# A streaming-encoder layer on one core: weight sums made by adding DMAs are issued one at a time over three stages, and a gate uses Silu in place of Sigmoid and a multiplication

## The chip, the cores and the metric

The kernel runs on one core of a Trainium2 chip. The metric is the device time of one execution in microseconds (us). Lower is better. Names of engines in the profile: PE is TensorE (matmuls; PEld is its weight load), DVE is VectorE, ACT is ScalarE, POOL is GpSimd, and SP is SyncE, which issues most DMAs.

## The reference, cut to what matters

One layer over 1024 frames of width 1024. The change touches how two things are computed: the weighted sums that feed the projections `W_out` and `w_ffn_down`, and the SwiGLU gate.

```python
merged = (jax.nn.sigmoid(gate_a) * (oa @ w_branch_a[li])
          + jax.nn.sigmoid(gate_b) * (ob @ w_branch_b[li]))
x = x + merged @ w_out[li]
h2 = rmsnorm(x, norm_ffn_g[li])
x = x + (jax.nn.silu(h2 @ w_ffn_gate[li]) * (h2 @ w_ffn_up[li])) @ w_ffn_down[li]
h3 = rmsnorm(x, norm_ple_g[li])
x = x + jax.nn.sigmoid(h3 @ w_ple_gate[li]) * (p[li] @ w_ple_proj[li])
```

## The kernel before

Everything is held with features on the partitions and frames along the free axis, in tiles of 128 x 512 or 128 x 1024. A float32 product is made of three fast products: each operand is split into a high part (a cast to `fp32r`, on ScalarE) and a low part (the rest, a subtraction on VectorE or GpSimd), and a block product is hi x hi, lo x hi and hi x lo. In the names below, `whi`/`wlo` and `wh`/`wl` are the high and low parts of weights, `wr` the raw weights as loaded, `q` a sum or difference of weight blocks, `pm` a PSUM bank, `t` a 128 x 512 temporary from a ring of eight, `s` a 128 x 1024 slot, `rb` the row of norm factors, `d` a tile in device memory.

The stages in order of time: norm, recurrent mixer, attention, gate units, branches, output projection, gate/up units of the feed-forward, its down projection, embedding. From the gate units on, products of 2 x 2 blocks are made by Strassen's scheme, seven products in place of eight. A *unit* of the gate units or of the gate/up units (`strassen`, line 1429) is seven products of 12 matmuls of 128 x 512 each; the result of the fourth goes onto the bank of the second, so the sum `u2 = p1 + b2` on VectorE must have read that bank first (lines 1457 to 1465).

The seven products need seven forms of the weights. For a unit, `strassen_weights` (line 1386) makes those of the *next* unit as side work: sums and differences `q` on VectorE, high parts on ScalarE, low parts on GpSimd and (one of them) on VectorE. It is a generator; after each product the unit takes one step of it. There are 12 gate-unit column blocks in six units (`gate_units`, line 800; they make the sigmoids of `gate_a` and `gate_b`), and 22 gate/up units: unit 0 is `first_part` and `second_part`, units 1 to 21 are the loop in `ff_pairs` (line 1515). Even units make the gate, odd ones the up half.

A gate unit's four results pass through `unit_gate` (line 1372): VectorE multiplies by the norm row into a slot `s` (twice its half), ScalarE makes the Sigmoid in a temporary `t`, and GpSimd multiplies twice, `s*t` and then `s*rb`. In the up unit VectorE multiplies the result in (`unit_up`).

For `W_out` and `w_ffn_down` the sums of weights are made in device memory, without an engine reading them: `dma_sums` (line 1053) first copies blocks of the weight into spill tiles (SP queue, during attention), then issues DMAs from the GpSimd queue that add a second block onto the copy in transit (`accum_op`). There are 8 such additions for `W_out` (`self.osum`) and 24 for `w_ffn_down` (`self.wsum`). Each `next()` of these generators issues one. Those of `osum` go out in the gate units, two to a unit, until they are used up; those of `wsum` in the up units 1, 3, 5, ... of the feed-forward, three to a unit, until they are used up in unit 15. `drain` issues what is left before the sums are used.

What sets the order: the framework schedules an engine's instructions freely, except those that go through `self.V`, `self.A`, `self.G`, `load` or `mul`, which are kept in program order on their engine (`Pinned`, line 45). The additions in transit go through `self.G`. The low parts of ordinary weights (`unit_piece`, line 118) and the additions of the two branch products (`branches`, line 893) are free on GpSimd. In `branches` eight weight tiles are used, one for 48 matmuls; weights are made ready three tiles ahead.

Of the kernel before, what the change touches and what calls it, by code (L numbers as in the profile page):

```python
# [14 lines left out]
ALU = mybir.AluOpType  # L15
# [40 lines left out]
class Trunk:  # L56
    def __init__(self, tc, d, out):
        self.tc, self.nc, self.d, self.out = tc, tc.nc, d, out
        self.V = Pinned(self, self.nc.vector, "dve")
        self.A = Pinned(self, self.nc.scalar, "act")  # L60
        self.G = Pinned(self, self.nc.gpsimd, "pool")
        self.n = self.turn = 0
        self.by_turns = False
        self.ahead = 2
        self.done = set()
        self.prev = {}
# [9 lines left out]
    def load(self, out, ap):  # L76
        return self.order(self.nc.sync.dma_start(out, ap), "sp")
# [40 lines left out]
    def unit_piece(self, unit, a, b):  # L118
        hi, lo, raw, ap = unit
        c = slice(a, b)  # L120
        self.load(raw[:, c], ap[:, c])
        self.nc.scalar.copy(hi[:, c], raw[:, c])  # L122
        self.turn += 1
        rest = self.nc.vector if self.by_turns and self.turn % 2 else self.nc.gpsimd
        rest.tensor_tensor(lo[:, c], raw[:, c], f32(hi[:, c]), ALU.subtract)  # L125

    def weights(self, n=1, ahead=AHEAD):
# [672 lines left out]
    def gate_units(self):  # L800

        V, A = self.V, self.A
        h0, h1 = slice(0, HALF), slice(HALF, T)
        self.gd = [self.spill() for _ in range(2 * KC)]
        self.kept = []
        for k in (2, 3):
            self.mix_load(k, self.slot(), [self.stmp(), self.stmp()])
        self.strassen_load()
        side = chain(self.strassen_weights(V), self.mix_sums(2), self.mix_sums(3))
        ts, self.gates = self.gates, []  # L810
        for c, t in enumerate(ts):
            A.activation(t, t, AF.Sigmoid)
            self.kept.append((self.gd[c], t))
        for c in range(2, PLAIN):
            (w,) = self.weights(1, ahead=PLAIN - 1 - c)
            for half in range(2):
                if c == PLAIN - 1 and half:
                    drain(side)
                    side = self.mix_last()
                stream = self.feature(w, self.u, half, piece=2)  # L820
                while True:
                    try:
                        next(stream)
                    except StopIteration as e:
                        ps = e.value
                        break
                    next(side, None)
                    if c == 2 and half == 0 and self.kept:
                        self.keep_heads(self.ob, self.obd, [2, 3])
                        self.gate_keep()  # L830
                    next(side, None)
                self.gate_done(c, half, ps)
                next(side, None)
        drain(side)
        u, t = self.u, self.t32
        cut = lambda pair, h: [x[:, h] for x in pair]
        four = range(4)
        self.sops = [
            [cut(u[2 * k + 1], h1) for k in four], [cut(t[k], h1) for k in four],
            [cut(self.t1[k // 2], slice(k % 2 * HALF, k % 2 * HALF + HALF)) for k in four], [cut(t[k], h0) for k in four],  # L840
            [cut(u[2 * k], h1) for k in four], [cut(u[2 * k + 1], h0) for k in four], [cut(u[2 * k], h0) for k in four]]
        units = (2 * KC - PLAIN) // 2
        for n in range(units):

            def side():
                more = self.strassen_weights() if n + 1 < units else self.branch_first()
                if n == 0:
                    yield
                    yield
                next(more, None)  # L850
                if n + 2 < units:
                    self.strassen_load()
                yield
                for i, _ in enumerate(more):
                    if i % 2:
                        next(self.osum, None)
                    yield

            self.strassen(lambda c, half, ps: self.gate_done(PLAIN + 2 * n + c, half, ps), side(), early=n == 0)
            yield 0  # L860
        self.gate_keep()

    def branch_load(self, src):
        raws = []
# [28 lines left out]
    def branches(self):  # L893
        nc, V = self.nc, self.V
        self.m = {}
        gates, load = self.bgates, self.gate_load

        def tile(c, half):
            key = f"B{c % 2 + 1}{half + 1}", c // 4
            if key not in self.m:  # L900
                self.m[key] = self.slot()
            return self.m[key][:, c // 2 % 2 * HALF:c // 2 % 2 * HALF + HALF]

        src = self.osrc
        for dd in range(4):
            (w,) = self.weights()
            load()
            if dd == 1:
                raws = self.branch_load(self.obd)
                late = []  # L910
            for i in range(2):
                c = 2 * dd + i
                for half in range(2):
                    hs = slice(half * HALF, half * HALF + HALF)
                    ps = yield from self.feature(w, src, half, off=i * HALF)
                    V.tensor_tensor(tile(c, half), ps, gates[c][:, hs], ALU.mult)
                    yield 2592
                if dd > 1:
                    late.append(self.split(raws[len(late)]))
        src = late  # L920
        for dd in range(4):
            (w,) = self.weights()
            load()
            for i in range(2):
                c = 2 * dd + i
                g = gates[KC + c]
                for half in range(2):
                    hs = slice(half * HALF, half * HALF + HALF)
                    ps = yield from self.feature(w, src, half, off=i * HALF)
                    V.tensor_tensor(g[:, hs], ps, g[:, hs], ALU.mult)  # L930
                    (nc.gpsimd if dd < 3 else V).tensor_tensor(tile(c, half), tile(c, half), g[:, hs], ALU.add)
                    yield 2592
            if dd == 1:
                self.branch_sums(0)
            if dd == 2:
                self.x, self.xd = [], [None] * KC
                for c in range(KC):
                    x = self.slot()
                    self.load(x, self.d["x"][c])
                    self.x.append(x)  # L940
                self.m_order = [(b, i) for _, b in self.KINDS for i in range(2)]
                self.m_ready = []
                self.m_split()
# [150 lines left out]


    def out_proj(self):
        drain(self.osum)
        split, ready = self.m_split, self.m_ready

        def operand(b, i):  # L1100
            got = ready.pop(0)
            if len(ready) < 2:
                split()
            return got

        split()
        self.branch_sums(1)
        self.by_turns = True
        yield from self.passes(4, operand, self.added(lambda c: self.x[c]), self.ffn_side())
        self.by_turns = False  # L1110
# [261 lines left out]
    def unit_gate(self, c, half, ps):  # L1372
        V, A, G = self.V, self.A, self.G
        g = self.gu[c]
        hs = slice(half * HALF, half * HALF + HALF)
        s = self.stmp()
        V.tensor_tensor(g[:, hs], ps, self.rb[:, hs], ALU.mult)
        A.activation(s, g[:, hs], AF.Sigmoid)
        G.tensor_tensor(g[:, hs], g[:, hs], s, ALU.mult)
        G.tensor_tensor(g[:, hs], g[:, hs], self.rb[:, hs], ALU.mult)  # L1380

    def unit_up(self, c, half, ps):
        hs = slice(half * HALF, half * HALF + HALF)
# [131 lines left out]
    def ff_pairs(self):  # L1515
# [5 lines left out]
        for n in range(1, units):  # L1521
# [3 lines left out]
            def side():  # L1525
# [6 lines left out]
                yield  # L1532
                for i, _ in enumerate(more):
                    next(keep, None)
                    if n % 2 and i % 2 == 0:
                        next(self.wsum, None)
                    yield
                drain(keep)

# [5 lines left out]
    def down_plan(self):  # L1545

        n = NFF // 2
        self.aorder = [(b, i, min(D, n * HALF - i * D)) for _, b in self.KINDS for i in range(STEPS)]
        drain(self.wsum)
        self.plan_weights(self.quad_plan(self.d["dw"], n, self.sums) + self.worder2)  # L1550
        self.anext, self.araw, self.aready = 0, [], []

# [366 lines left out]
def drain(stream):  # L1919
    while True:  # L1920
        try:
            next(stream)
        except StopIteration as e:
            return e.value
# [114 lines left out]
```

## Time and profile before

| | |
|---|---|
| median of three runs | 1601.0 us (1599.59 to 1601.37) |
| the profiled execution | 1600.6 us, its span 1598.8 us, mean granted clock 0.994 |
| attention ends, gate units begin | about 518 us into the span |
| branches, output projection | about 667 to 755, 755 to 860 |
| gate/up units | about 860 to 1290 |
| down projection, embedding | about 1290 to 1510, 1510 to 1599 |

In a row of a group of instructions stand line, engine, operation, output<-inputs with shapes, the count, then busy us and mean ns of one, then the idle time of the engine just before them with what ended it. In a row of the timeline stand start and length in us, and in brackets the idle time before. An "issue" as releaser means that the engine waited for nothing that the profile shows. Many instructions share line 53, which is the helper that pins them; they are told apart by their tiles. In a row of a stretch stand the stretch, then busy us and the number of instructions for PE, PEld, DVE, ACT and POOL, the granted clock of PE as a share of full speed, the mean busy share of the DMA engines, and GB/s.

### The profile page before, as it was taken

Reading aid. Unit: us, or ns where it says so; the run is one execution under the profiler, and the core shown is the slowest. Engines: PE = TensorE matmul, PEld = TensorE weight load, DVE = VectorE, ACT = ScalarE, POOL = GpSimd, SP = SyncE. Lnnn points to the kernel's source line nnn. Section 1 sums busy time; section 2 is a strip of 40 time slices with the busy share of each in tenths; the row PEclk is TensorE's granted clock in tenths of the full one; section 3 lists DMA queues with packets and bytes.
Section 4 is the critical chain, followed back from the end, with each engine's and each line's share of the span. In section 5 each row is a group of like instructions: output and inputs, shape, how many; then the busy total and the mean of one; then the engine's idle time right before and its main releaser. Section 6 shows DMA issues by size and latency. Waiting matters only on the chain.

```text
span 1598.8 us, 21535 instructions
## 1 busy us (share of the span) xinstructions
PE 1559.1 (98%) x8224; PEld 1312.8 (82%) x8224; DVE 1171.8 (73%) x1685; ACT 636.9 (40%) x1057; POOL 712.5 (45%) x397
## 2 busy tenths in 40 slices
PE   8999999999999999999999999989999999999997
PEld 6998998888888888888888777877788888888886
DVE  5656656378786876436898889889998876765677
ACT  5222221177676633322566222222222234445462
POOL 3422221313121053335313777767777764544453
PEclk9999999999999999999999999999999999999998
DMA  5101000362523475754335555555543278885434
GB/s 187 53 28 50 31 28 27 112 185 80 177 82 118 170 174 130 271 203 184 114 136 211 137 133 141 123 132 135 129 132 103 78 267 325 294 283 184 133 116 164
DMA packets 83527, 230.38 MB, mean 144 GB/s; under 512 B 8928, under 2 KB 9568, under 8 KB 82912
## 3 DMA queue, kind: packets, MB, share of 16 engines
q1 hardware_dynamic: 76880, 213.26, 39.1%
q0 software_dynamic: 6400, 15.73, 6.1%
q8 instruction: 64, 1.05, 0.3%
q14 instruction: 39, 0.32, 0.1%
q10 hardware_dynamic: 144, 0.02, 0.0%
HBM read 179.43 MB, written 81.00 MB: 163 GB/s over the span
## 4 chain that ended last, share of the span: by engine, by line
PE 75%; DVE 15%; issue 3%; ACT 1%; DMA 1%; POOL 1%; SPq 0%; DVEq 0%; POOLq 0%; ACTq 0%
PE pm L82 72%; DVE s L53 8%; DVE q L53 3%; PE pm L85 3%; DVE t L53 2%; DVE m L53 1%; DMA d<-s 1%; DVE pm L53 0%; ACT s L53 0%; POOL wl L125 0%; DMA wr<-in_fm 0%; ACT wh L122 0%; POOL m L555 0%; ACT m L53 0%; DVE wlo L53 0%
## 5 line engine op out<-in xcount | busy, mean ns | idle before, releaser
L82 PE MATMUL pm<-s,wh 128*128 128x512 f32 (+1 forms) x1712 | 531.9, 392 | 6.6 <-ACT wh L122 5.3
L82 PE MATMUL pm<-s,whi 128*128 128x512 f32 x1568 | 487.8, 392 | 14.4 <-DVE t L53 14.4
L125 POOL TENSOR_TENSOR wl<-wr,wh 128x1024 fp32r<-128x1024 f32 (+2 forms) x108 | 266.9, 2476 | 396.7 <-ACT wh L122 383.4
L82 PEld LDWEIGHTS pm<-s,wh 128*128 128x128 f32 x1712 | 319.9, 189 | 73.4 <-ACT wh L122 5.9
L82 PEld LDWEIGHTS pm<-s,whi 128*128 128x128 f32 x1568 | 295.1, 189 | 81.6 <-DVE t L53 20.7
L82 PE MATMUL pm<-s,wl 128*128 128x512 f32 (+1 forms) x856 | 333.9, 390 | 0.0
L53 DVE TENSOR_TENSOR s<-s,s 128x512 f32<-128x512 f32 (+3 forms) x228 | 273.2, 1230 | 79.2 <-ACT s L53 41.7
L82 PE MATMUL pm<-s,wlo 128*128 128x512 f32 x784 | 307.0, 392 | 0.7 <-POOL wlo L53 0.7
L82 PE MATMUL pm<-wh,s 128*128 128x256 f32 (+1 forms) x896 | 237.6, 340 | 0.0
L122 ACT CAST wh<-wr 128x1024 fp32r<-128x1024 f32 (+2 forms) x114 | 115.0, 1010 | 271.8 <-PE pm L82 139.4
L82 PEld LDWEIGHTS pm<-s,wl 128*128 128x128 f32 x856 | 161.3, 188 | 33.7 <-POOL wl L125 0.6
L82 PEld LDWEIGHTS pm<-s,wlo 128*128 128x128 f32 x784 | 148.0, 189 | 33.0 <-POOL wlo L53 1.6
L82 PEld LDWEIGHTS pm<-wh,s 128*128 128x128 f32 x896 | 154.4, 190 | 14.0
L53 DVE TENSOR_TENSOR t<-pm,t 128x512 f32<-128x512 f32 x138 | 94.5, 685 | 79.7 <-PE pm L82 75.2
L82 PE MATMUL pm<-wl,s 128*128 128x256 f32 (+1 forms) x448 | 147.5, 329 | 0.4 <-POOL wl L125 0.4
L53 POOL TENSOR_TENSOR wlo<-wr,whi 128x512 fp32r<-128x512 f32 (+1 forms) x53 | 113.4, 2142 | 73.4 <-PE pm L82 67.2
L53 ACT CAST whi<-q 128x512 fp32r<-128x512 f32 (+1 forms) x81 | 61.4, 758 | 153.2 <-DVE q L53 113.1
L53 ACT CAST s<-s 128x1024 fp32r<-128x1024 f32 (+1 forms) x94 | 90.1, 980 | 63.4 <-DVE s L53 34.7
L53 POOL TENSOR_TENSOR wlo<-q,whi 128x512 fp32r<-128x512 f32 x52 | 84.5, 1625 | 50.4 <-DVE t L53 17.8
L53 POOL TENSOR_TENSOR s<-s,t 128x512 f32<-128x512 f32 x44 | 73.1, 1662 | 66.6 <-ACT t L53 66.6
L82 PEld LDWEIGHTS pm<-wl,s 128*128 128x128 f32 x448 | 85.4, 191 | 5.9 <-POOL wl L125 0.6
L53 ACT ACTIVATE t<-s 128x512 f32<-128x512 f32 x44 | 27.8, 632 | 142.8 <-DVE s L53 139.0
(145 smaller groups left out, 1929.7 us busy)
## 6 DMA issues: line engine op xcount, KB each, us to landing
s<-d SPq DMA_DIRECT2D x67, 512.0 KB, 6.1
d<-s SPq DMA_DIRECT2D x87, 256.0 KB, 2.5
wr<-d SPq DMA_DIRECT2D x36, 512.0 KB, 3.8
wr<-in_sg SPq DMA_DIRECT2D x22, 512.0 KB, 5.1
wr<-in_su SPq DMA_DIRECT2D x22, 512.0 KB, 4.2
s<-in_x SPq DMA_DIRECT2D x21, 512.0 KB, 7.5
d<-in_wq SPq DMA_DIRECT2D x20, 512.0 KB, 9.6
d<-s SPq DMA_DIRECT2D x18, 512.0 KB, 5.1
```

The costliest lines, as they stand in the source:

```text
L53: return lambda *a, **k: self.trunk.order(op(*a, **k), self.key)
L82: return self.order(self.nc.tensor.matmul(*a, **k))
L85: return self.order(self.nc.tensor.transpose(*a, **k))
L122: self.nc.scalar.copy(hi[:, c], raw[:, c])
L125: rest.tensor_tensor(lo[:, c], raw[:, c], f32(hi[:, c]), ALU.subtract)
```

## The change

Three edits.

1. The two generators of additions are chained (`self.adds`). Two are issued in each of the six gate units (12), one at each weight tile of the branches (8), and one in each gate/up unit from unit 3 on, at the last step of the side work but one, until they are used up (12, in units 3 to 14).
2. `unit_gate` takes Silu on ScalarE into the temporary `t` and multiplies once on GpSimd, `t*rb` into `s`. The scheme of table loads then has two more of them.
3. In the branches the low parts of the weights and the additions of the branch products go through `self.G`, so that they stand in program order with the additions in transit.

```diff
-        rest = self.nc.vector if self.by_turns and self.turn % 2 else self.nc.gpsimd
+        rest = self.nc.vector if self.by_turns and self.turn % 2 else self.G if self.pinned else self.nc.gpsimd
...
+        self.adds = chain(self.osum, self.wsum)
         for n in range(units):
...
                 for i, _ in enumerate(more):
                     if i % 2:
-                        next(self.osum, None)
+                        next(self.adds, None)
                     yield
...
         self.gate_keep()
+        self.pinned = True
...
             (w,) = self.weights()
+            next(self.adds, None)
             load()
...
-                    (nc.gpsimd if dd < 3 else V).tensor_tensor(tile(c, half), tile(c, half), g[:, hs], ALU.add)
+                    (self.G if dd < 3 else V).tensor_tensor(tile(c, half), tile(c, half), g[:, hs], ALU.add)
...
     def out_proj(self):
-        drain(self.osum)
+        self.pinned = False
...
         V.tensor_tensor(g[:, hs], ps, self.rb[:, hs], ALU.mult)
-        A.activation(s, g[:, hs], AF.Sigmoid)
-        G.tensor_tensor(g[:, hs], g[:, hs], s, ALU.mult)
-        G.tensor_tensor(g[:, hs], g[:, hs], self.rb[:, hs], ALU.mult)
+        A.activation(s, g[:, hs], AF.Silu)
+        G.tensor_tensor(g[:, hs], s, self.rb[:, hs], ALU.mult)
...
                     next(keep, None)
-                    if n % 2 and i % 2 == 0:
-                        next(self.wsum, None)
+                    if i == 4 and n > 2:
+                        next(self.adds, None)
                     yield
                 drain(keep)
...
-        drain(self.wsum)
+        drain(self.adds)
```

GpSimd's order in up unit 3 and the beginning of gate unit 4, before the change; `d` is the spill tile that an addition in transit writes:

```order
L53 DMA d_3925<-in_wq 256x1x512
L53 TENSOR_TENSOR wlo_8861<-wr_8659,whi_8860 128x1024
L53 DMA d_3639<-d_3462 128x1024
L53 TENSOR_TENSOR wlo_8880<-q_8841,whi_8879 128x512
L53 DMA d_4029<-d_3846 128x1024
L53 TENSOR_TENSOR wlo_8931<-q_8913,whi_8930 128x512
L53 TENSOR_TENSOR wlo_8957<-wr_8823,whi_8956 128x512
L53 TENSOR_TENSOR s_8935<-s_8935,t_9018 128x512
L53 TENSOR_TENSOR s_8935<-s_8935,rb_8393 128x512
L53 TENSOR_TENSOR wlo_9001<-wr_8825,whi_9000 128x1024
```

and in a later pair of the changed kernel, from the end of an up unit into the gate unit after it:

```order
L53 TENSOR_TENSOR wlo_9171<-q_9133,whi_9170 128x512
L53 DMA d_4436<-d_4377 128x1024
L53 TENSOR_TENSOR wlo_9221<-q_9203,whi_9220 128x512
L53 TENSOR_TENSOR wlo_9247<-wr_9115,whi_9246 128x512
L53 TENSOR_TENSOR s_9225<-t_9311,rb_8405 128x512
L53 TENSOR_TENSOR wlo_9294<-wr_9117,whi_9293 128x1024
L53 TENSOR_TENSOR s_9224<-t_9332,rb_8405 128x512
L53 TENSOR_TENSOR wlo_9316<-q_9274,whi_9315 128x512
L53 TENSOR_TENSOR s_9225<-t_9353,rb_8405 128x512
L53 DMA d_4718<-d_4647 128x1024
L53 TENSOR_TENSOR s_9224<-t_9381,rb_8405 128x512
L53 TENSOR_TENSOR wlo_9386<-q_9357,whi_9385 128x512
```

Three additions in an up unit have become one, ahead of the unit's last low part; a gate unit, which had none, has one ahead of its last multiplication; and each pair of multiplications, the second of which reads what the first wrote, is one.

GpSimd's order from the last gate units into the branches, before the change (the first two rows belong to the fifth gate unit, `wl` are the branch weights):

```order
L53 TENSOR_TENSOR wlo_6565<-wr_6388,whi_6564 128x1024
L53 TENSOR_TENSOR wlo_6587<-q_6546,whi_6586 128x512
L53 TENSOR_TENSOR wlo_6645<-q_6625,whi_6644 128x512
L125 TENSOR_TENSOR wl_6665<-wr_6667,wh_6666 128x1024
L125 TENSOR_TENSOR wl_6671<-wr_6673,wh_6672 128x1024
L125 TENSOR_TENSOR wl_6677<-wr_6679,wh_6678 128x1024
L125 TENSOR_TENSOR wl_6821<-wr_6823,wh_6822 128x1024
```

and of the changed kernel:

```order
L53 DMA d_3462<-in_wq 256x1x512
L53 TENSOR_TENSOR wlo_6565<-wr_6388,whi_6564 128x1024
L53 TENSOR_TENSOR wlo_6588<-q_6546,whi_6587 128x512
L53 DMA d_3846<-in_wq 256x1x512
L53 TENSOR_TENSOR wlo_6647<-q_6627,whi_6646 128x512
L53 DMA d_3539<-in_wq 256x1x512
L125 TENSOR_TENSOR wl_6667<-wr_6669,wh_6668 128x1024
L53 DMA d_3925<-in_wq 256x1x512
L125 TENSOR_TENSOR wl_6673<-wr_6675,wh_6674 128x1024
L125 TENSOR_TENSOR wl_6679<-wr_6681,wh_6680 128x1024
L53 TENSOR_TENSOR wl_6825<-wr_6827,wh_6826 128x1024
L53 DMA d_3639<-d_3462 128x1024
```

Four additions now stand among the last low parts of the gate units and the first branch weights, where there was none; the order of the rest is the same. The order on PE, DVE and SP is the same in both kernels.

More of the change, by code (lines that the diff above doesn't have):

```diff
@@ L62, in __init__ @@
         self.n = self.turn = 0
-        self.by_turns = False
+        self.by_turns = self.pinned = False
         self.ahead = 2
@@ L1534, in side @@
                     next(keep, None)
-                    if n % 2 and i % 2 == 0:
-                        next(self.wsum, None)
+                    if i == 4 and n > 2:
+                        next(self.adds, None)
                     yield
```

## The prediction

> **What bounds the kernel now.** I read the busy times first, then the stretches, then what TensorE (PE) waits for, then the instructions around those waits.
>
> ```profile
> PE 1559.1 (98%) x8224; PEld 1312.8 (82%) x8224; DVE 1171.8 (73%) x1685; ACT 636.9 (40%) x1057; POOL 712.5 (45%) x397
> 518.00:720.00 202.00, 202.00 (x922) 167.04 (x921) 124.87 (x155) 75.97 (x107) 62.53 (x40) 1.00 0.60 188
> 920.00:960.00 40.00, 36.55 (x155) 29.51 (x154) 35.81 (x31) 10.79 (x16) 29.75 (x20) 0.96 0.52 137
> 1040.00:1080.00 40.00, 35.37 (x146) 28.69 (x145) 33.58 (x33) 10.89 (x16) 27.23 (x19) 0.91 0.54 138
> 1248.00:1287.00 39.00, 38.99 (x172) 32.30 (x173) 31.13 (x30) 12.62 (x18) 28.18 (x18) 1.00 0.29 102
> ```
>
> The columns of the four stretches are PE, weight loads, VectorE (DVE), ScalarE (ACT) and GpSimd (POOL), then granted clock, DMA share and GB/s. PE is full in the gate units and most of the branches (518 to 720) and in the last gate/up pairs (1248 to 1287). It loses time in the gate/up units that issue additions in transit (up to about 1190), and there the clock falls too. What it waits for from 880 on is one thing, a sum on DVE:
>
> ```profile
> PE pm L82 <- DVE t L53: 14.4, 14, 4.6
> PE pm L82 <- POOL wlo L53: 0.7, 2, 0.6
> 883.63 0.74 PE L82 MATMUL pm<-s,whi 128*128 128x512 f32 x2 [1.28 <-DVE t L53]
> 925.00 1.22 PE L82 MATMUL pm<-s,whi 128*128 128x512 f32 x2 [2.50 <-DVE t L53]
> 946.68 0.73 PE L82 MATMUL pm<-s,whi 128*128 128x512 f32 x2 [0.95 <-DVE t L53]
> 1048.98 1.22 PE L82 MATMUL pm<-s,whi 128*128 128x512 f32 x2 [4.63 <-DVE t L53]
> 1110.15 0.73 PE L82 MATMUL pm<-s,whi 128*128 128x512 f32 x2 [0.57 <-DVE t L53]
> 1150.43 0.74 PE L82 MATMUL pm<-s,whi 128*128 128x512 f32 x2 [1.19 <-DVE t L53]
> 1209.23 0.73 PE L82 MATMUL pm<-s,whi 128*128 128x512 f32 x2 [0.42 <-DVE t L53]
> 925.00 9.88 PE pm L82 x36
> 966.43 8.48 PE pm L82 x36
> 1048.98 24.54 PE pm L82 x96
> 1005.96 22.08 PE pm L82 x96
> ```
>
> The fourteen waits fall on the fourth product of a unit, whose bank is free only when `u2 = p1 + b2` has read it. Six are shown (sum 11.1 us); the other eight, the 0.42 at 1209.23 for one, are 0.41 to 0.44 each and make up the rest (3.3 us). The last four rows are pieces of the chain: after the 2.50 and the 4.63 wait the same matmuls took 1.4 and 2.5 us longer than elsewhere. That is the lower clock, 3.9 us more.
>
> Why is the sum late? Here are DVE and GpSimd before the 4.63 wait, then at a unit without additions:
>
> ```profile
> 1019.26 0.68 DVE L53 TENSOR_TENSOR q<-wr,wr 128x512 f32<-128x512 f32 x1
> 1021.23 1.06 POOL L53 DMA_DIRECT2D d<-in_wq  x1 [4.44 <-issue]
> 1029.91 1.06 POOL L53 DMA_DIRECT2D d<-in_wq  x1 [6.29 <-issue]
> 1030.51 1.80 POOL L53 TENSOR_TENSOR wlo<-q,whi 128x512 fp32r<-128x512 f32 x1
> 1031.77 1.78 POOL L53 TENSOR_TENSOR wlo<-wr,whi 128x512 fp32r<-128x512 f32 x1
> 1033.02 1.77 POOL L53 TENSOR_TENSOR s<-s,t 128x512 f32<-128x512 f32 x1
> 1030.13 5.22 DVE L53 TENSOR_TENSOR s<-s 128x512 f32<-128x512 f32 x1
> 1205.09 1.78 DVE L53 TENSOR_TENSOR q<-wr,wr 128x512 f32<-128x512 f32 x1
> 1206.28 1.75 POOL L53 TENSOR_TENSOR s<-s,t 128x512 f32<-128x512 f32 x1
> 1206.91 1.67 DVE L53 TENSOR_TENSOR q<-q,wr 128x512 f32<-128x512 f32 x1
> 1208.11 1.61 POOL L53 TENSOR_TENSOR s<-s,rb 128x512 f32<-128x512 f32 x1
> ```
>
> A DVE operation that reads SBUF alone takes 0.68 us when GpSimd rests (first row). Beside a running GpSimd operation it ends about 0.55 us after that one ends: 1.67 to 1.78 us. Two things make that worse. An addition sits on the GpSimd queue for 4 to 6 us before it goes out ("issue", nothing the profile shows), when the previous one is only 8.7 us old; the work behind it piles up. Then the pile runs back to back, 1.26 us from start to start, and DVE does not get in between: its 128x512 operation from 1030.13 took 5.22 us, through three of them. In the unit without additions DVE slips in once per GpSimd operation, and only 0.42 us is lost.
>
> By the Trainium skill, SBUF — State Buffer, Who interferes with whom, a DVE instruction with two SBUF inputs and a GpSimd instruction that reads SBUF exclude each other for one whole instruction. The trace agrees on the 1.67 us, not on the 5.22 us, which is longer than any GpSimd instruction beside it. By that rule alone an addition costs DVE no more than any neighbour does, and the 1.0 us that the sum below leaves for the remaining additions would be 0.
>
> **The change, part by part.** *Additions.* Gate/up units lose 12 of 24 additions; the other 12 come one to a unit, about 19 us apart, behind the last difference (`q4`) of the weights' side work. At that distance none should queue behind another, so the 11.1 us and the clock's 3.9 us go. The first of the six waits (1.28 us, at 883.63) comes in an up unit before any addition, from the GpSimd backlog of the first gate block; that backlog halves (next term). For what the 12 still cost I have two bounds: nothing (the 202 us row held eight additions without one PE wait) and 0.95 us each, as in the wait at 946.68, so 11.4 us. I take 1.0 us in all, near the first row, since the additions now mostly stand ahead of work that waits for ScalarE or PE.
>
> *The multiplication.*
>
> ```profile
> L53 POOL TENSOR_TENSOR s<-s,rb 128x512 f32<-128x512 f32 x44 | 73.8, 1676 | 3.5
> L53 POOL TENSOR_TENSOR s<-s,t 128x512 f32<-128x512 f32 x44 | 73.1, 1662 | 66.6 <-ACT t L53 66.6
> L53 ACT ACTIVATE t<-s 128x512 f32<-128x512 f32 x44 | 27.8, 632 | 142.8 <-DVE s L53 139.0
> L53 ACT ACT_TABLE_LOAD x2 | 2.6, 1283 | 0.0
> ```
>
> The 44 `s<-s,t` go: 73.1 us of GpSimd time, none of it on PE's path by itself. What it buys is fewer collisions at the start of an up unit, where the two `q` sums precede `u2`. There the gate unit's last six GpSimd operations become three. The eight small waits (3.3 us) can go wholly or stay; I take half, 1.7 us left. The 0.7 us that PE waits for a GpSimd `wlo` lies behind the same pairs and goes.
>
> *The table.* ScalarE gets the same 44 activations with another function (632 ns; no row shows a Silu, I keep 632) and two table loads, one ahead of the first gate, one ahead of the embedding's first Sigmoid.
>
> ```profile
> 867.91 0.63 ACT L53 ACTIVATE t<-s 128x512 f32<-128x512 f32 x1 [2.16 <-DVE s L53]
> 1543.82 1.18 ACT L53 ACTIVATE pm<-pm 128x512 f32<-128x512 f32 x2 [3.47 <-DVE pm L53]
> ```
>
> ScalarE idles 2.16 and 3.47 us at these places, longer than 1.283 us; and even where the load comes only after the wait, the first is paid back by the multiplication that no longer follows (1.66 us on average). I take 0; bounds 0 and 2.6 us. The Trainium skill, ScalarE: Activation LUTs, What ACT_TABLE_LOAD costs, speaks against the change: 1283 ns for the load, as the row has it, and about 1380 ns of drain for each switch. By that the sum would be up to 5.3 us worse, if both switches were exposed.
>
> *Four additions in the last gate units, eight in the branches.* In the gate units they repeat what the 202 us row held. One spot is tight: the last gate unit's second addition now stands ahead of the second and third branch weights on GpSimd.
>
> ```profile
> 651.42 4.76 POOL L125 TENSOR_TENSOR wl<-wr,wh 128x1024 fp32r<-128x1024 f32 x2 [1.89 <-ACT wh L122]
> 658.32 2.49 POOL L125 TENSOR_TENSOR wl<-wr,wh 128x1024 fp32r<-128x1024 f32 x1 [2.14 <-ACT wh L122]
> 659.53 2.36 DVE L192 TENSOR_TENSOR s<-s,s 128x1024 fp32r<-128x1024 f32 x1 [0.99 <-ACT s L191]
> 670.08 0.69 DVE L53 TENSOR_TENSOR s<-pm,s 128x512 f32<-128x512 f32 x1 [1.05 <-PE pm L82]
> ```
>
> If it waits like the one at 1021.23, the second weight (653.8, half of the first row) slips to about 659 and the third behind it, beside DVE's splits of the branch input, which PE needs from about 667 (the last row reads its first finished sum, twelve matmuls of 0.23 us after the start). The weights themselves are 8 us or more early. DVE can be held by one more 2.5 us operation. I take 1.0 us; bounds 0 and 4 (2.5 us and a clock loss like the 1.4 us above). In the branches one addition comes each 10.9 us, and DVE's products there read PSUM and take 0.69 us beside GpSimd or not: 0.
>
> GpSimd's additions into the branch tiles keep their order among the weights; program order moves nothing there but the additions in transit. The end of the kernel has a few casts and subtractions swapped, with no PE wait near: 0.
>
> **Sum.** Gain 11.1 + 3.9 + 0.7 + (3.3 - 1.7) - 1.0 - 1.0 = 15.3 us. The profiled execution took 1600.6 us (span 1598.8), so 1585.3; the median of the runs is 0.4 us above that execution: about 1585.5 us. All waits gone is 19.0 us, 1581.6. The costs at their upper bounds (11.4, 3.3, 2.6, 4) leave next to nothing.
>
> **Rivals.** *Spread, not removed* (0.13). Each of the 12 additions keeps a wait like 0.95 us. For: that wait followed a single late addition. Against: eight additions in the gate units cost none. Gain 15.3 - 10.4 = 4.9 us: 1596.
>
> *A new wait where the branches begin* (0.09), the 4 us and their like once more at a later weight: gain 15.3 - 7 = 8 us: 1593.
>
> *DVE is shut out by the shorter queue* (0.09; slower). The pair `s<-s,t`, `s<-s,rb` depended on itself: the second waited for the first, and in that gap DVE slipped in. Without pairs, GpSimd's operations can run at the 1.26 us pitch seen behind additions, and DVE waits through two more, 2.5 us in each of 11 up units: 27.5 us lost against 15.7 (11.1, 3.9, 0.7) gained, about 1613. It decides from 1.4 us per up unit on. For: the 5.22 us row. Against: between dependent gate multiplications and other work there are waits for ScalarE, and there is less work.
>
> *Nothing gained* (0.05): the clock and `u2` are late for another reason, DVE's own load of 31 us in 39 us without additions: 1600. Against it: PE's 38.99 in that very stretch.
>
> **How the numbers follow.** The forecast has 0.64, with its own range 1581.5 to 1590. Holding most of the next two cases, 8 in 10 lie in 1581.5 to 1594. A difference under 0.2% (3 us) can't be told from none. Faster: 0.64 + 0.13 + 0.09 = 0.86; same 0.05; slower 0.09.
>
> **What would show it.** Right: PE's wait on DVE `t` falls from 14.4 to below 4 us in all, none over 1 us; every 40 us stretch from 920 to 1250 at clock 1.00; no "issue" idle of 4 us before GpSimd's DMAs in the gate/up units; DVE operations over 3 us gone there; POOL about 70 us less busy. Wrong: PE below full between 650 and 760, waits of 1 us or more in units that follow a gate unit, or a PE wait on ScalarE near 868 or 1544.

## The result, and the profile after

The changed kernel takes 1583.9 us in the median of six runs (1581.05 to 1587.71); the kernel before 1601.2 us (1599.59 to 1604.26, six runs). The ratio (of means, here and below) is 0.989, with a 95% interval of 0.9874 to 0.9907. The profiled execution has a span of 1581.7 us, 17.1 us below that of the kernel before.

What PE waits for from the gate units on, in the changed kernel (waits in all, how many, the longest), and the places of the waits that bear on the prediction:

```profile
PE pm L82 <- DVE t L53: 2.4, 2, 2.1
PE pm L82 <- DVE s L192: 0.9, 2, 0.8
PE pm L82 <- ACT s L191: 0.4, 1, 0.4
886.12 1.13 PE L82 MATMUL pm<-s,whi 128*128 128x512 f32 x2 [2.13 <-DVE t L53]
1269.05 0.73 PE L82 MATMUL pm<-s,whi 128*128 128x512 f32 x2 [0.24 <-DVE t L53]
```

Of the fourteen waits on the sum `u2` (14.4 us) two are left. The first up unit's has grown from 1.28 to 2.13 us: PE comes there earlier, since its wait of 0.57 us on a GpSimd `wlo` just before is gone, and VectorE does not. New are the waits on `s` of lines 191 and 192, at the first branch product.

The stretches, with columns as before, of the changed kernel:

```profile
640.00:700.00 60.00, 58.63 (x255) 47.40 (x254) 27.92 (x30) 18.14 (x23) 22.34 (x14) 1.00 0.95 307
880.00:920.00 40.00, 37.87 (x160) 30.88 (x159) 31.28 (x31) 10.79 (x16) 24.47 (x14) 0.96 0.26 91
1040.00:1080.00 40.00, 40.00 (x178) 33.14 (x177) 31.07 (x33) 11.46 (x17) 25.25 (x16) 1.00 0.44 119
```

The clock of 0.96 from 880 to 920 lies behind the wait of 2.13 us. From 1040 to 1080 PE runs 178 matmuls where it ran 146, at a clock of 1.00 where it was 0.91. GpSimd's total falls from 712.5 to 647.5 us. In the gate/up units no GpSimd DMA is preceded by an idle "issue" any more, and no single VectorE operation of 128 x 512 takes over 2.9 us (before, twelve took 3.1 to 5.2 us).

### The profile page after: what moved, and what is told of

Read it like the earlier page. It is cut to its first block, busy times and chain, and to the rows that moved or that the text cites. A ratio compares the mean times of both kernels' runs of the same rounds, so it can differ in the third digit from the quotient of the medians.

```text
span 1581.7 us, 21492 instructions
## 1 busy us (share of the span) xinstructions
PE 1553.5 (98%) x8224; PEld 1311.6 (83%) x8224; DVE 1106.2 (70%) x1685; ACT 638.7 (40%) x1059; POOL 647.5 (41%) x353
## 4 chain that ended last, share of the span: by engine, by line
PE 78%; DVE 9%; DMA 2%; POOL 2%; ACT 2%; issue 2%; SPq 0%; DVEq 0%; ACTq 0%; POOLq 0%
PE pm L82 76%; DVE s L53 6%; PE pm L85 3%; DVE m L53 1%; POOL wl L125 1%; DMA wr<-d 1%; ACT s L53 1%; DMA s<-d 1%; ACT wh L122 1%; POOL s L53 1%; DVE q L53 0%; DVE t L53 0%; DMA wr<-in_ba 0%; DMA wr<-in_dw 0%; DVE wl L125 0%
## 5 line engine op out<-in xcount | busy, mean ns | idle before, releaser
L125 POOL TENSOR_TENSOR wl<-wr,wh 128x1024 fp32r<-128x1024 f32 (+2 forms) x100 | 248.5, 2495 | 361.3 <-ACT wh L122 346.9
L53 DVE TENSOR_TENSOR s<-s,s 128x512 f32<-128x512 f32 (+3 forms) x228 | 281.9, 1269 | 79.1 <-ACT s L53 41.5
L53 POOL TENSOR_TENSOR s<-t,rb 128x512 f32<-128x512 f32 x44 | 71.6, 1627 | 98.8 <-ACT t L53 98.8
```

Of the source, the lines that this page charges most:

```text
L53: return lambda *a, **k: self.trunk.order(op(*a, **k), self.key)
```

## The experiments

Each run's time is a median beside the kernel before on the same chip. "Silu only", "spread only" and so on are short names for the kernels.

**Spread only.** The changed kernel with the gate as before:

```diff
-        A.activation(s, g[:, hs], AF.Silu)
-        G.tensor_tensor(g[:, hs], s, self.rb[:, hs], ALU.mult)
+        A.activation(s, g[:, hs], AF.Sigmoid)
+        G.tensor_tensor(g[:, hs], g[:, hs], s, ALU.mult)
+        G.tensor_tensor(g[:, hs], g[:, hs], self.rb[:, hs], ALU.mult)
```

> The kernel before with the additions spread and pinned as in the change, but Sigmoid and two GpSimd multiplications kept. Theory (the clusters of three additions make the big waits and the clock loss, the multiplication pairs make the small ones): PE's wait on DVE t is 4 to 7 us (the first, 1.3 us, and the 0.41 us ones stay), the clock stays at 1.00 in every stretch from 920 to 1250, no DVE 128x512 operation over 3.2 us there; time 1586 to 1591. Rival (GpSimd's load by the pairs is the cause): the wait stays above 10 us and the time above 1595.

1590.7 us against 1599.6 (ratio 0.9947, 0.9932 to 0.9962). PE waits on DVE `t`:

```profile
PE pm L82 <- DVE t L53: 5.1, 10, 1.3
888.18 0.73 PE L82 MATMUL pm<-s,whi 128*128 128x512 f32 x2 [1.30 <-DVE t L53]
926.98 0.73 PE L82 MATMUL pm<-s,whi 128*128 128x512 f32 x2 [0.42 <-DVE t L53]
1237.61 0.74 PE L82 MATMUL pm<-s,whi 128*128 128x512 f32 x2 [0.42 <-DVE t L53]
```

One wait of 1.30 and nine of 0.42 us, one in each up unit from 3 to 19 (unit 21, the last, makes no sums for a next unit). The big waits are gone and the small ones stay, as the theory had it. A small wait costs PE more than the figure in brackets: from 926.98 to 1237.61 eight pairs of units take 38.83 us each, in the changed kernel a pair takes 38.08 (the VectorE operation `s<-s,s` that starts at 951.21 comes again at 989.29). That is 0.75 us for each wait of 0.42 and some 6.8 us for the nine, which is all that this kernel is slower than the changed one.

**Silu only.** The kernel before with edit 2 alone:

```diff
-        A.activation(s, g[:, hs], AF.Sigmoid)
-        G.tensor_tensor(g[:, hs], g[:, hs], s, ALU.mult)
-        G.tensor_tensor(g[:, hs], g[:, hs], self.rb[:, hs], ALU.mult)
+        A.activation(s, g[:, hs], AF.Silu)
+        G.tensor_tensor(g[:, hs], s, self.rb[:, hs], ALU.mult)
```

> The kernel before with Silu and one GpSimd multiplication, additions in clusters of three as before. Theory: the small waits of 0.41 us go, but DVE operations over 3 us stay beside the clusters (eight or more), GpSimd still stands idle 2 to 6 us for no shown reason ahead of additions, and PE waits 4 to 9 us on DVE t; time 1589 to 1596. Rival (the pairs are the cause): the wait falls below 3 us as in the changed kernel, time 1582 to 1586.

1580.6 us against 1599.6 (0.9884, 0.9865 to 0.9902). The theory falls: with the clusters in place PE waits 2.5 us, not 4 to 9, and the time lies even below the rival's range. Here are PE's waits, then GpSimd and VectorE behind the three additions ahead of what was the 4.63 us wait before, now in this kernel:

```profile
PE pm L82 <- DVE t L53: 2.5, 2, 2.1
1013.46 1.06 POOL L53 DMA_DIRECT2D d<-in_wq  x1 [4.18 <-issue]
1022.13 1.07 POOL L53 DMA_DIRECT2D d<-in_wq  x1 [6.29 <-issue]
1023.99 1.78 POOL L53 TENSOR_TENSOR wlo<-wr,whi 128x512 fp32r<-128x512 f32 x1
1027.73 1.30 POOL L53 TENSOR_TENSOR s<-t,rb 128x512 f32<-128x512 f32 x1 [1.97 <-ACT t L53]
1038.23 1.74 POOL L53 TENSOR_TENSOR s<-t,rb 128x512 f32<-128x512 f32 x1 [1.30 <-ACT t L53]
1037.41 0.68 DVE L53 TENSOR_TENSOR q<-wr,wr 128x512 f32<-128x512 f32 x1
1038.12 0.69 DVE L53 TENSOR_TENSOR q<-q,wr 128x512 f32<-128x512 f32 x1
1045.41 4.38 DVE L53 TENSOR_TENSOR s<-t,s 128x512 f32<-128x512 f32 x1
```

The queue is held up as before, 4.2 and 6.3 us, and VectorE still has operations of 4.3 to 4.6 us (six of them, the last row is one). But GpSimd is idle again 1.97 and 1.30 us ahead of multiplications of the gate unit that follows, waiting for ScalarE, and the two `q` sums ahead of the up unit's `u2` take 0.7 us each. In the kernel before, GpSimd had no idle time from 1029.9 to past 1051, and the same sums took 1.6 to 1.8 us. These sums and the 20 us behind the additions, first of the kernel before, then the 20 us of Silu only:

```profile
1044.89 1.75 DVE L53 TENSOR_TENSOR q<-wr,wr 128x512 f32<-128x512 f32 x1
1046.68 1.64 DVE L53 TENSOR_TENSOR q<-q,wr 128x512 f32<-128x512 f32 x1
1030.00:1050.00 20.00, 15.37 (x67) 12.37 (x66) 19.90 (x15) 6.19 (x10) 19.69 (x13) 0.94 0.50 132
```

```profile
1023.00:1043.00 20.00, 20.00 (x89) 16.54 (x89) 17.20 (x17) 6.45 (x10) 16.73 (x11) 1.00 0.51 133
```

GpSimd is busy 19.7 of 20 us in the one, 16.7 in the other. A gate unit lasts 19 us: before, it could not work off a late start within it.

**The multiplication twice.** If that is so, the load alone must bring the waits back. Silu only, with its multiplication done a second time onto the same result:

```diff
         G.tensor_tensor(g[:, hs], s, self.rb[:, hs], ALU.mult)
+        G.tensor_tensor(g[:, hs], s, self.rb[:, hs], ALU.mult)
```

> The Silu-only kernel (additions in clusters of three) with its one GpSimd multiplication done twice into the same place, so that GpSimd has its former load and its second multiplication again follows the first. Theory (the waits need both: the clusters hold the queue up, and only with the pairs' load is GpSimd too full in a gate unit to catch up before the up unit's sums): the waits of the kernel before come back, 10 to 15 us on DVE t with one above 3 us, clock below 0.98 in a stretch, 1595 to 1602 us. Rival (something else of the Silu path, the ScalarE order or the tiles, took the waits away): wait below 5 us, 1580 to 1587 us.

1598.4 us against 1599.3 (1.0001, 0.9992 to 1.001); the waits are back. Here are their sum, the two largest, each behind three additions in a row that read the weight itself (`in_wq`), and a stretch:

```profile
PE pm L82 <- DVE t L53: 12.4, 13, 4.4
924.19 0.74 PE L82 MATMUL pm<-s,whi 128*128 128x512 f32 x2 [2.50 <-DVE t L53]
1047.78 0.73 PE L82 MATMUL pm<-s,whi 128*128 128x512 f32 x2 [4.43 <-DVE t L53]
1040.00:1080.00 40.00, 35.57 (x150) 28.92 (x149) 36.16 (x33) 10.89 (x16) 28.26 (x18) 0.96 0.55 144
```

GpSimd is again busy 19.7 of 20 us from 1029 to 1049. So it is not the activation function or the tiles, but the second multiplication on GpSimd. The run brings back its time and its place behind the first together; the two were not tried apart.

**The addition two steps earlier.** The changed kernel with `i == 2` for `i == 4` in the gate/up units.

> The changed kernel with the one addition of each gate/up unit two steps earlier, between two low-part subtractions of which the second is ready (a12, then s3), in place of ahead of work that still waits. Theory (an addition between ready GpSimd operations lets them run on without a gap for DVE): DVE 128x512 operations of 3.5 to 4.2 us come back in six or more units, PE's wait on DVE t rises from 2.4 us to 3 to 8 us, time 1584 to 1592. Rival (only the distance from one addition to the next counts): no such operations, wait 2 to 3 us, time within 2 us of the changed kernel.

1583.8 us against 1599.6 (0.9903, 0.9888 to 0.9918), the time of the changed kernel. VectorE operations of 2.7 us come in six units, none of 3.5 us or more, and PE waits 2.3 us. The rival holds for the time: at this load the place does not matter.

**Free order on GpSimd.** The changed kernel without its third edit:

```diff
-        rest = self.nc.vector if self.by_turns and self.turn % 2 else self.G if self.pinned else self.nc.gpsimd
+        rest = self.nc.vector if self.by_turns and self.turn % 2 else self.nc.gpsimd
...
-                    (self.G if dd < 3 else V).tensor_tensor(tile(c, half), tile(c, half), g[:, hs], ALU.add)
+                    (nc.gpsimd if dd < 3 else V).tensor_tensor(tile(c, half), tile(c, half), g[:, hs], ALU.add)
```

> The changed kernel with the branch weights' low parts and the branch additions not pinned on GpSimd: the scheduler then puts the eight additions of the branches in one row ahead of the second to the sixth branch weight. Theory (program order is what keeps them one to a weight tile): GpSimd stands in front of the additions, each waiting for earlier ones to land, some 7 to 8 us for each from the second or third on, so the second branch weight's low part comes 30 to 50 us late against a lead of some 10 to 20 us; PE waits 15 to 40 us on POOL wl early in the branches and the time is 1600 to 1630. Rival (the queue takes eight additions without waiting): each costs 1 us of GpSimd, no PE wait beyond 2 us, time 1582 to 1588.

1599.9 us against 1599.6 (1.0006, 0.9996 to 1.0015): all of the gain is gone. GpSimd and PE in the branches, in the slowest of the ten executions (1604.5 us):

```profile
692.31 1.07 POOL L53 DMA_DIRECT2D d<-in_wq  x1 [10.51 <-issue]
702.53 1.04 POOL L53 DMA_DIRECT2D d<-in_wq  x1 [9.15 <-issue]
709.12 1.05 POOL L53 DMA_DIRECT2D d<-in_wq  x1 [5.55 <-issue]
712.59 0.79 PE L82 MATMUL pm<-s,wl 128*128 128x512 f32 x1 [7.07 <-POOL wl L125]
```

Six of the eight additions of the branches now stand in one row (the other two go before them, with one branch weight between). GpSimd waits up to 10.5 us ahead of one, and a branch weight comes 7.1 us late, not 15 to 40 us as the theory had it; further waits on VectorE's splits add 7.9 us, and PE's clock is 0.86 from 660 to 745.

**Changed and Silu only, side by side**, on one chip, together with the two kernels that follow.

> The changed kernel itself, beside the Silu-only kernel on one chip. Theory (with Silu alone PE no longer waits in the gate/up units, so the spread additions gain nothing there, and they cost some 1.4 us where the branches begin): 1 to 3 us above the Silu-only kernel. Rival (the 3 us between the two in separate jobs are scatter, or the spread still gains): equal within 1 us, or below it.

> The kernel before with Silu and one multiplication, additions in clusters, once more. Theory: 1578 to 1583 us, 1 to 3 us below the changed kernel; no PE wait near 667, the first up unit's wait of 2.1 us stays. Rival: equal to the changed kernel within 1 us.

1584.3 us (1583.38 to 1590.54) and 1580.1 us (1578.64 to 1581.41), against 1600.4 before: once Silu is in, the kernel with the spread additions is 4.2 us slower, and its fastest execution is behind the slowest of Silu only. Silu only has no wait near 667. Its wait in the first up unit, 2.1 us in the first profile, is not in this one.

**No addition in the last gate unit.** The changed kernel with

```diff
-                    if i % 2:
+                    if i % 2 and n + 1 < units:
                         next(self.adds, None)
```

> The changed kernel without additions in the last gate unit (the chain then ends two gate/up units later). Theory (the addition ahead of two ready branch weights lets GpSimd run on and holds VectorE's split of the branch input): the waits near 667 (1.4 us) go, and VectorE's operation of 4.7 us there is one of 0.7 us; span 1.4 to 2 us below the changed kernel. Rival (the DMA traffic of the additions delays the branch input): the waits stay above 0.8 us.

1579.9 us (1578.11 to 1580.45). At the beginning of the branches, first GpSimd and VectorE of the changed kernel, then of this one:

```profile
656.80 5.27 POOL L125 TENSOR_TENSOR wl<-wr,wh 128x1024 fp32r<-128x1024 f32 x2
657.96 4.67 DVE L53 TENSOR_TENSOR t<-t,rb 128x512 f32<-128x512 f32 x1
669.10 0.50 PE L82 MATMUL pm<-s,wh 128*128 128x512 f32 x1 [0.77 <-DVE s L192]
```

```profile
657.74 2.40 POOL L125 TENSOR_TENSOR wl<-wr,wh 128x1024 fp32r<-128x1024 f32 x1 [2.21 <-ACT wh L122]
657.15 0.69 DVE L53 TENSOR_TENSOR t<-t,rb 128x512 f32<-128x512 f32 x1
640.00:700.00 60.00, 60.00 (x266) 49.53 (x265) 27.34 (x33) 20.21 (x25) 23.29 (x14) 1.00 0.90 298
```

With the addition ahead of two ready branch weights, GpSimd ran both back to back and VectorE's operation lasted through them, 4.67 us; without it 0.69 us, and PE does 266 matmuls between 640 and 700 in place of 255. At 0.226 us each (60 us for 266) that is 2.5 us; the medians differ by 4.4 us. The profiled executions of the two kernels on this chip differ by 4.4 us too (spans of 1582.9 and 1578.5), but 2.9 of that is there already at 550 us (the same matmul starts at 552.28 and at 549.42), ahead of the first addition. So scatter between executions is as large as the effect, and only the 2.5 us are shown to come from the edit.

**The first up unit's sums later.** Silu only, and in that unit alone the next weights' sums `q` are formed after `u2`:

```diff
         self.A.copy(p1, b1)
-        next(side, None)
+        if not late:
+            next(side, None)
...
         next(side, None)
+        if late:
+            next(side, None)
...
-            self.strassen((self.unit_gate, self.unit_up)[n % 2], side())
+            self.strassen((self.unit_gate, self.unit_up)[n % 2], side(), late=n == 1)
```

> The Silu-only kernel, and in the first up unit alone the two weight sums q come after the sum u2 on VectorE, not ahead of it. Theory (the 2.1 us wait there is u2 queued behind two q sums that GpSimd holds up): that wait goes to below 0.3 us and the span is 1.5 to 2.5 us below the Silu-only kernel. Rival (u2 is late because the gate's own work on VectorE is late): a wait of 1 us or more stays.

1579.2 us (1578.24 to 1582.58), not told apart from Silu only. PE's waits in this unit, and VectorE's `u2`:

```profile
885.44 0.73 PE L82 MATMUL pm<-s,whi 128*128 128x512 f32 x2 [0.67 <-DVE t L53]
892.28 0.73 PE L82 MATMUL pm<-s,whi 128*128 128x512 f32 x2 [1.11 <-DVE t L53]
884.69 0.69 DVE L53 TENSOR_TENSOR t<-pm,t 128x512 f32<-128x512 f32 x1 [1.74 <-ACT t L53]
```

The wait for `u2` falls from 2.13 to 0.67 us: the two sums made most of it. What is left is neither below 0.3 us, as the theory had it, nor 1 us or more, as the rival had it: `u2` now waits for `p1`, which ScalarE copies behind the last gate's Silu. The second wait is new. It is at the sixth product, whose bank `u3 = p1 + b2` must have read, and VectorE comes to `u3` only at 891.55, behind the sums that the edit moved.

The wait is also not the same in each execution of one kernel. Here is the stretch ahead of it in the two profiles of Silu only, the first with the wait of 2.13 us, the second without:

```profile
850.00:872.00 22.00, 21.74 (x113) 18.53 (x112) 18.87 (x22) 17.35 (x28) 3.97 (x3) 1.00 0.43 148
850.00:872.00 22.00, 21.74 (x106) 18.32 (x105) 19.77 (x24) 17.43 (x25) 6.16 (x4) 0.92 0.49 163
```

Where the wait is missing, PE had just lost seven matmuls to a lower clock and came later. So what the wait itself costs is open.

**Both.** The changed kernel with the last two edits together.

> The changed kernel without additions in the last gate unit, and the first up unit's q sums after u2. Theory (from the two runs alone: 1579.9 and 1579.2 us, and both leave only single waits of about 1 us in the gate/up units): 1578 to 1580 us, no wait near 667, 1 to 2 us on DVE t. Rival: the second edit gives nothing, 1580 us and 2 us on DVE t.

1578.9 us (1578.37 to 1580.2) against 1599.3, ratio 0.9875 (0.9858 to 0.9891). In its profile one wait on DVE `t` is left in the gate/up units, 0.36 us, but there too the clock from 850 to 872 is 0.92, as in the Silu-only profile without the wait, so the second edit can't be credited with it. It is the fastest median, though within the scatter of Silu only, of the kernel without the last gate unit's additions and of the one with the sums later. Each of these four is some 4 to 5 us below the changed kernel's 1584.3 (this one on another chip).

## Why the prediction was right, point by point

The time (1585.5 us forecast, 1583.9 measured) and most of its mechanism held. The division between the edits did not, and that the total came so near is in part luck. Here are two matmuls that both kernels have, one shortly ahead of the gate/up units and one at the start of the embedding, first before the change, then after:

```profile
857.61 0.50 PE L82 MATMUL pm<-ph,wh 128*128 128x512 f32 x1 [0.26 <-DVE m L214]
1513.66 1.16 PE L82 MATMUL pm<-eye,m 128*128 128x128 f32 x8 [0.56 <-POOL m L1703]
```

```profile
860.11 0.50 PE L82 MATMUL pm<-ph,wh 128*128 128x512 f32 x1 [0.26 <-DVE m L214]
1496.61 1.16 PE L82 MATMUL pm<-eye,m 128*128 128x128 f32 x8 [0.55 <-POOL m L1706]
```

Between them lie 656.1 and 636.5 us: 19.6 us gained, where the sum had 16.3 (11.1 + 3.9 + 0.7 + 1.6 - 1.0). Ahead of them 2.5 us are lost, where the sum had 1.0. The two errors partly cancel.

Two of the prediction's own signs of being wrong came: PE is not full between 650 and 760 (the waits near 667), and an up unit, the first, has a wait of over 1 us (2.13). That wait also breaks its sign of being right, "none over 1 us". In its arithmetic, 1585.3 and 0.4 are 1585.7, and the costs at their upper bounds add up to 21.3 us, 2.3 more than the whole gain of 19.0.

- *Big waits and clock, 11.1 and 3.9 us, go with the clusters of additions.* They went, but for the first (below), and spreading alone does take them away (spread only). But the step took the clusters to be enough to make them. They need two things at once: a queue held up by additions close together, and a gate unit in which GpSimd has no time to catch up. Either edit breaks that, so the gains do not add: 8.9 us from spreading, 19.0 from Silu, 16.0 to 17.3 from both (medians, each beside the kernel before on the same chip). The step that failed is "what it buys is fewer collisions at the start of an up unit", sized at 1.6 us of the small waits and 0.7 us: Silu alone bought nearly all 14.4 us and the clock.
- *Half of the 3.3 us of small waits stays.* 0.24 us stayed. The step chose the middle between two ends without a row for it. Spread only keeps a wait of 0.42 us in the up units from 3 to 19 and Silu only has none of them, so the multiplication pairs made them. The term was also too small: at the 0.75 us that spread only shows for each, the eight were worth some 6 us (an estimate).
- *The first of the big waits (1.28 us) goes.* It was 2.13 us in the profile, with a lower clock behind it: mis-seen, since removing the `wlo` wait ahead of it only moved PE into it.
- *The 12 additions left in the gate/up units cost 1.0 us.* They cost nothing that PE shows, at either of the two places tried.
- *1.0 us where the branches begin.* Right in the mechanism down to the operation (predicted: VectorE held by one more 2.5 us operation; measured: 4.67 us through two), but mis-sized: 1.4 us of waits in brackets, and 2.5 us of PE's work missing.
- *The table loads cost nothing.* Shown: the first ran from 868.28 to 869.56, and ScalarE was then still idle 0.86 us, waiting for VectorE; after the second it idled 2.17 us more. In the second profile of Silu only ScalarE was not idle there:

```profile
867.10 0.59 ACT L229 COPY rb<-pm 128x512 f32<-128x512 f32 x1 [0.31 <-PE pm L82]
867.71 1.28 ACT L53 ACT_TABLE_LOAD   x1
869.00 0.63 ACT L53 ACTIVATE t<-s 128x512 f32<-128x512 f32 x1
```

The load begins 0.02 us after the copy and the activation 0.01 us after the load. The 1380 ns of drain that the Trainium skill states beside the load (ScalarE: Activation LUTs, What ACT_TABLE_LOAD costs) are not there; the measurement decides.
- *Program order moves nothing but the additions.* True of the two orders compared, yet incomplete: without it the scheduler puts six of the additions in one row, and 16 us are lost.
- *VectorE shut out by the shorter queue* (the rival on the slow side) did not come in the up units. VectorE held through GpSimd operations without a gap is what happened where the branches begin.

## What to carry to other kernels

When two causes together make a wait, a sum of terms can come near the total with the wrong parts: run each edit alone before keeping both. Here one edit alone was faster than all three. Look at whether an engine off the critical path can work off a delay within one unit of the loop; here 19.7 us of work in 20 us could not, and 16.7 us could. Look at what stands behind an asynchronous transfer that shares a compute engine's queue. One ahead of two ready operations cost PE time where the branches begin, and six in a row cost all of the gain; in the gate/up units neither the place nor, with Silu, three in an up unit cost anything that PE shows.

## What was not expected of the hardware

In these traces VectorE stayed shut out while ready GpSimd operations followed one another behind a DMA issue: 4.67 us through two weight subtractions, 5.22 us through three short ones. The Trainium skill (SBUF — State Buffer, Who interferes with whom) speaks of an exclusion for one whole instruction; the runs show more than one. Of three additions that read the weight itself within 17 us, the second waits about 4 us before it is issued and the third 6 to 7 us, and one of six in a row waits 10.5 us; what they wait for was not tried.
